# Attention times value on one core: output stores moved into the ring of the loads, and one more unit loaded in halves

## The chip, the cores and the metric

The kernel runs on one core of a Trainium2 chip. The metric is the device time of one execution in microseconds (us). The time of a run is some 2 us above the span of its profile (1064.05 against 1062.3 in the profiled run of the kernel before), which goes from the first to the last instruction.

## The reference

```python
# attn_weights: (8, 12, 1024, 1024) float32; v: (8, 12, 1024, 64) float32
return np.einsum('bhqs,bhsd->bhqd', attn_weights, v).astype(np.float32)
```

403 MB of attention weights and 25 MB of V are read, and 25 MB of output are written.

## The kernel before

Two heads make one unit ("pair"), so there are NP = 48 units. A unit's weights (8 MB of float32 in HBM) are loaded by a casting DMA that GpSimd issues, as 4 MB of bf16, into one of two buffers. PE transposes them, multiplies with V and transposes the result back; the unit's output (512 KB: 128 rows of 4 KB) is stored by a DMA that SP issues. In the profile the packets of the loads are on queue 0 (11520 packets; "the ring" in this document) and those of SP's DMAs on queue 1 (7520); the page counts 16 DMA engines.

```python
    HELD = 7
    MARK = 11
    chunks_of = {                          # how a unit's load is cut, in sixteenths
        NP - 3: [(0, GH), (GH, GH)],       # halves
        NP - 2: [(g, DG) for g in range(0, G, DG)],                       # quarters
        NP - 1: [(0, 4), (4, 4), (8, 4), (12, 2), (14, 1), (15, 1)],
    }
    o_pool = ctx.enter_context(tc.tile_pool(name="op", bufs=3 + HELD))
    # ... other pools cut

    def load_attn(ip):
        abf = abf_pool.tile([P, G, S], bf16)
        abf_of[ip] = abf
        for g0, gn in chunks_of.get(ip, [(0, G)]):
            nc.gpsimd.dma_start(
                out=abf[:, ds(g0, gn)].rearrange("p g s -> p (g s)"),
                in_=attn_p[ip][:, ds(g0 * S, gn * S)],
            )

    def store(ip, osb):
        nc.sync.dma_start(
            out=out_p[ip].rearrange("p g d -> p (g d)"),
            in_=osb.rearrange("p g d -> p (g d)"),
        )

    def store_held(abf, g):                # 7 stores wait for part of the last load
        mark = const_pool.tile([1, P], bf16)
        waits = nc.sync.dma_start(out=mark, in_=abf[0:1, g, 0:P])
        with tc.issue_after(waits.ins):
            for ip in sorted(held):
                store(ip, held.pop(ip))

    def pair(ip):                          # units 0 to 44
        # ... buffers cut
        for g in range(G):
            transpose_g(abf, at, g)
        load_ahead(ip)                     # the load of unit ip + 2 (and V every other time)
        # ... multiply, copies, transpose back cut
        if ip < NP - 1 - HELD:
            store(ip, osb)
        else:
            held[ip] = osb

    def direct_pair(ip, behind):           # units 45 to 47, a quarter at a time
        # ... cut
        if ip == NP - 1:
            store_held(abf, MARK)
        # ... per quarter: transposes, multiply, copies; unit 47 stores its pieces by SP
        load_ahead(ip)
        if ip < NP - 1:
            held[ip] = osb
```

Of the kernel before, what the change touches and what calls it, by code (L numbers as in the profile page):

```python
# [10 lines left out]
def kernel(  # L11
# [13 lines left out]
    nc = tc.nc  # L25
    fp32 = mybir.dt.float32
    bf16 = mybir.dt.bfloat16
# [4 lines left out]
    NP = NH // 2  # L32
    P = 128
    HP = P // 2
    G = Q // HP
    GH = G // 2
# [5 lines left out]
    NV = NH // VH  # L42


    HELD = 7
    MARK = 11
    DG = 4
    LAST = 3
    chunks_of = {
        NP - 3: [(0, GH), (GH, GH)],  # L50
        NP - 2: [(g, DG) for g in range(0, G, DG)],
        NP - 1: [(0, 4), (4, 4), (8, 4), (12, 2), (14, 1), (15, 1)],
# [8 lines left out]
    const_pool = ctx.enter_context(tc.tile_pool(name="const", bufs=1))  # L61
# [2 lines left out]
    vr_pool = ctx.enter_context(tc.tile_pool(name="vr", bufs=2))  # L64
    vbf_pool = ctx.enter_context(tc.tile_pool(name="vbf", bufs=4))
    ot_pool = ctx.enter_context(tc.tile_pool(name="ot", bufs=2))
    o_pool = ctx.enter_context(tc.tile_pool(name="op", bufs=3 + HELD))
    pt_pool = ctx.enter_context(tc.tile_pool(name="pt", bufs=4, space=bass.MemoryType.PSUM))
    po_pool = ctx.enter_context(tc.tile_pool(name="po", bufs=2, space=bass.MemoryType.PSUM))
    px_pool = ctx.enter_context(tc.tile_pool(name="px", bufs=2, space=bass.MemoryType.PSUM))  # L70
# [32 lines left out]
    def load_attn(ip):  # L103
        abf = abf_pool.tile([P, G, S], bf16)
        abf_of[ip] = abf
        for g0, gn in chunks_of.get(ip, [(0, G)]):
            nc.gpsimd.dma_start(  # L107
                out=abf[:, ds(g0, gn)].rearrange("p g s -> p (g s)"),
                in_=attn_p[ip][:, ds(g0 * S, gn * S)],
            )  # L110

    def load_first_v():
        v32 = const_pool.tile([P, VB, SB * D], fp32)
        nc.sync.dma_start(out=v32.rearrange("p b x -> p (b x)"), in_=v_g[0])
        vr = vr_pool.tile([P, VB, SB * D], bf16)
        vr_of[0] = vr
        nc.vector.tensor_copy(out=vr, in_=v32)  # L117

    def load_v(iv):
        vr = vr_pool.tile([P, VB, SB * D], bf16)  # L120
        vr_of[iv] = vr
        nc.gpsimd.dma_start(out=vr.rearrange("p b x -> p (b x)"), in_=v_g[iv])  # L122
# [21 lines left out]
    def transpose_g(abf, at, g):  # L144
        pt = pt_pool.tile([P, KW, P], fp32)
        words = abf[:, g].bitcast(fp32).rearrange("p (c k) -> p k c", k=KW)
        for k in range(KW):
            nc.tensor.matmul(  # L148
                out=pt[:, k],
                lhsT=words[:, k],  # L150
                rhs=ident,
                is_transpose=True,
                start=(k == 0),
                stop=(k == KW - 1),
            )
        copy = nc.vector.tensor_copy if g % 8 in (0, 2, 4, 5, 7) else nc.scalar.copy
        copy(  # L157
            out=at[:, g].rearrange("c k j two -> c (k j two)"),
            in_=pt.rearrange("c k j -> c (k j)").bitcast(bf16),
        )  # L160
# [20 lines left out]
    def transpose_back(ot, o_halves, j0, jn):  # L181
        px = px_pool.tile([P, jn, P], fp32)
        for j in range(jn):
            last = nc.tensor.matmul(  # L184
                out=px[:, j],
                lhsT=ot[:, j0 + j].rearrange("p h q -> p (h q)"),
                rhs=ident,
                is_transpose=True,
                start=(j == 0),
                stop=(j == jn - 1),  # L190
            )
        nc.scalar.copy(  # L192
            out=o_halves[:, :, ds(j0, jn)].rearrange("p half j d -> p j half d"),
            in_=px.rearrange("p j (half d) -> p j half d", half=2),
        )
        return last

    held = {}

    def store(ip, osb):  # L200
        nc.sync.dma_start(
            out=out_p[ip].rearrange("p g d -> p (g d)"),
            in_=osb.rearrange("p g d -> p (g d)"),
        )

    def store_held(abf, g):

        mark = const_pool.tile([1, P], bf16)
        waits = nc.sync.dma_start(out=mark, in_=abf[0:1, g, 0:P])
        with tc.issue_after(waits.ins):  # L210
            for ip in sorted(held):
                store(ip, held.pop(ip))

    def pair(ip):
        abf = abf_of.pop(ip)
        at = at_pool.tile([P, G, KW, P, 2], bf16)
        vbf = vbf_of.pop(ip)
        po = [po_pool.tile([P, GH * HP], fp32, name="po") for h in range(2)]
        ot = ot_pool.tile([P, GH, 2, HP], fp32)
        osb = o_pool.tile([P, G, D], fp32)  # L220
        o_halves = osb.rearrange("p (half j) d -> p half j d", half=2)
# [4 lines that stand above are left out]
        for h in range(2):  # L226
            for half in range(2):
                multiply(at, vbf, po, h, half)
        to_sbuf(po, ot)
        if ip % 2 == 0 and ip // 2 + 1 < NV:  # L230
            spread_v(ip // 2 + 1)
        for j0 in (0, 4):
            last = transpose_back(ot, o_halves, j0, 4)
# [4 lines that stand above are left out]
        return last  # L238

    def direct_pair(ip, behind):  # L240

        abf = abf_of.pop(ip)
        at = at_pool.tile([P, G, KW, P, 2], bf16)
        vbf = vbf_of.pop(ip)
        osb = o_pool.tile([P, G, D], fp32)
        if ip == NP - 1:
            store_held(abf, MARK)
        for c0, cn in chunks_of[ip]:
            for g0 in range(c0, c0 + cn, DG):
                gn = min(DG, c0 + cn - g0)  # L250
                with tc.issue_after(behind.ins):
                    for g in range(g0, g0 + gn):
                        transpose_g(abf, at, g)
                px = px_pool.tile([P, gn, 2, D], fp32)
                for g in range(g0, g0 + gn):
                    n = 0
                    for kw in range(KW):
                        for par in range(2):
                            behind = nc.tensor.matmul(  # L259
                                out=px[:, g - g0].rearrange("p h d -> p (h d)"),  # L260
                                lhsT=at[:, g, kw, :, par],
                                rhs=vbf[:, 2 * kw + par].rearrange("p h d -> p (h d)"),
                                start=(n == 0),
                                stop=(n == SB - 1),
                            )
                            n += 1
                for h in range(2):
                    copy = nc.vector.tensor_copy if h == 0 else nc.scalar.copy
                    rows = ds(h * HP, HP)
                    copy(out=osb[rows, ds(g0, gn)], in_=px[rows, :, h])  # L270
                if ip == NP - 1 and g0 in stores_of:
                    gs = ds(*stores_of[g0])
                    nc.sync.dma_start(out=out_p[ip][:, gs], in_=osb[:, gs])
        load_ahead(ip)
        if ip < NP - 1:
            held[ip] = osb
        return behind

    def load_ahead(ip):


        nxt = ip + 2
        if nxt < NP:
            if nxt % 2 == 1 and (nxt + 1) // 2 < NV:
                load_v((nxt + 1) // 2)
            load_attn(nxt)

    load_attn(0)
    load_first_v()
    constants()  # L290
    load_v(1)
    load_attn(1)
    spread_v(0)
    for ip in range(NP - LAST):
        last = pair(ip)
    for ip in range(NP - LAST, NP):
        last = direct_pair(ip, last)
# [30 lines left out]
```

## Time and profile before

| | before |
|---|---|
| time, median (lowest to highest), as known at the prediction | 1065.76 us (1063.76 to 1065.77) |
| span of the profiled run | 1062.3 us |
| PE busy | 76% |
| loads in the ring, share of 16 DMA engines | 93.9% |
| SP's queue (stores, first V) | 6.5% |

From the page of the kernel before: busy time of PE with its share of the span, the DMA engines' busy tenths in 40 equal slices, and the queues (packets, MB, share of 16 engines' time).

```profile
PE 806.8 (76%) x5640; PEld 648.9 (61%) x5640; DVE 390.1 (37%) x590; ACT 399.0 (38%) x486; POOL 46.3 (4%) x89
...
DMA  9999999999999999999999999999999999999998
...
q0 software_dynamic: 11520, 213.39, 93.9%
q1 hardware_dynamic: 7520, 26.22, 6.5%
q8 instruction: 44, 0.72, 0.2%
q14 instruction: 12, 0.10, 0.0%
```

The DMA engines are the limit.

The chain of waits of the kernel before, from 840 us on (start, length, what):

```profile
960.75 29.60 DMA abf<-in_attn_weights_dram
990.34 0.14 issue
990.48 1.53 PE pt L148 x6
992.01 1.71 PE px L184 x8
993.71 7.73 PE pt L148 x58
1001.44 4.74 PE po L167 x32
...
1052.28 0.55 PE pt L148 x4
```

The fourth unit from the end lands whole at 990.34; from there the chain is PE work, with short copies between, until the end. PE is late, and so is the last load, which must wait until the transposes of unit 45 have freed its buffer. The timeline of GpSimd in the kernel before (start, length; in brackets the idle time before it and what ended that):

```profile
1024.38 3.18 POOL L107 DMA_DIRECT2D abf<-in_attn_weights_dram  x6 [20.53 <-PE pt L148]
```

Stretches of the tail of the kernel before. The last two columns are the DMA engines' mean busy share and the GB/s they wrote:

```profile
core 0: us, PE busy (x) PEld busy (x) DVE busy (x) ACT busy (x) POOL busy (x), PEclk, DMA share, GB/s
1022.00:1026.00 4.00, 4.00 (x53) 3.99 (x52) 2.49 (x5) 1.38 (x2) 1.62 (x4) 1.00 0.84 160
...
1050.00:1054.00 4.00, 3.70 (x52) 3.50 (x51) 2.25 (x4) 1.91 (x3) 0.00 (x0) 1.00 1.03 411
1054.00:1058.00 4.00, 2.51 (x28) 1.98 (x25) 0.93 (x4) 1.48 (x3) 0.00 (x0) 1.00 1.00 393
1058.00:1060.00 2.00, 0.62 (x8) 0.45 (x8) 0.62 (x2) 0.21 (x1) 0.00 (x0) 1.00 0.29 100
```

The engines dip to 0.84 at 1022 to 1026, and they drain the held stores at full share until 1058.

### The profile page before, as it was taken

The numbers are of one execution on the slowest core, as the hardware profiler recorded it, in microseconds if no ns is written. First come the engines' busy times: TensorE is split into PE (matmuls) and PEld (weight loads), VectorE is DVE, ScalarE is ACT, GpSimd is POOL, SyncE is SP. The second block draws the span as 40 slices with busy tenths as digits, with TensorE's granted clock in tenths as the row PEclk, the third lists the DMA queues.
The fourth block names the chain that finished last, engine by engine and source line by source line (L and its number), as shares of the span: only waits on it lengthen the run. The fifth ranks groups of instructions, "written<-read, shape, count | busy, mean of one in ns | idle before, by whom it ended". The sixth has DMA issues, their size and how long they took to land.

```text
span 1062.3 us, 12938 instructions
## 1 busy us (share of the span) xinstructions
PE 806.8 (76%) x5640; PEld 648.9 (61%) x5640; DVE 390.1 (37%) x590; ACT 399.0 (38%) x486; POOL 46.3 (4%) x89
## 2 busy tenths in 40 slices
PE   0988758787688876777668787788777877688797
PEld 0676546665567655665556655666556655577597
DVE  0353323433234333343334433344333433334354
ACT  0353324433244332443324433344333433334353
POOL 2000000000000000000000000000000000000010
PEclk9988878888888887888878888778877888878899
DMA  9999999999999999999999999999999999999998
GB/s 215 220 221 239 225 220 236 228 223 232 225 229 229 225 225 239 221 221 238 227 225 229 230 224 229 227 228 230 222 230 236 221 222 233 233 217 217 208 202 253
DMA packets 19096, 240.43 MB, mean 226 GB/s; under 512 B 2144, under 2 KB 2528, under 8 KB 12000
## 3 DMA queue, kind: packets, MB, share of 16 engines
q0 software_dynamic: 11520, 213.39, 93.9%
q1 hardware_dynamic: 7520, 26.22, 6.5%
q8 instruction: 44, 0.72, 0.2%
q14 instruction: 12, 0.10, 0.0%
HBM read 427.82 MB, written 25.17 MB: 426 GB/s over the span
## 4 chain that ended last, share of the span: by engine, by line
DMA 69%; issue 20%; PE 10%; DVE 0%; ACT 0%; POOLq 0%
DMA abf<-in_attn_weights_dram 69%; PE pt L148 6%; PE px L259 2%; PE px L134 1%; PE px L184 1%; PE po L167 0%; DVE vbf L142 0%; DVE at L157 0%; ACT at L157 0%; DVE osb L270 0%; ACT osb L270 0%; POOLq L107 0%; POOLq L122 0%; POOLq L77 0%; POOLq L312 0%
## 5 line engine op out<-in xcount | busy, mean ns | idle before, releaser
L148 PE MATMUL pt<-ident,abf 128*128 128x128 f32 x3072 | 455.2, 314 | 214.2 <-DMA abf<-in_attn_weights_dram 214.2
L148 PEld LDWEIGHTS pt<-ident,abf 128*128 128x128 f32 x3072 | 436.7, 214 | 232.8 <-issue 157.9
L157 DVE COPY at<-pt 128x1024 bf16<-128x1024 bf16 x480 | 319.0, 688 | 448.9 <-PE pt L148 446.2
L157 ACT COPY at<-pt 128x1024 bf16<-128x1024 bf16 x288 | 288.3, 1013 | 107.4 <-PE pt L148 106.5
L167 PE MATMUL po<-at,vbf 128*64 128x512 bf16 x1440 | 216.5, 391 | 0.0
L167 PEld LDWEIGHTS <-vbf 128*64 128x64 bf16 x1440 | 106.5, 108 | 92.9
L192 ACT COPY osb<-px 128x512 f32<-128x512 f32 x90 | 52.6, 585 | 276.5 <-PE px L184 276.4
L179 ACT COPY ot<-po 128x512 f32<-128x512 f32 x45 | 26.3, 585 | 191.4 <-PE po L167 191.4
L184 PE MATMUL px<-ident,ot 128*128 128x128 f32 x360 | 84.5, 396 | 17.4 <-DVE vbf L142 17.4
L184 PEld LDWEIGHTS px<-ident,ot 128*128 128x128 f32 x360 | 69.3, 211 | 28.7 <-DVE vbf L142 28.7
L142 DVE CAST vbf<-px 128x512 bf16<-128x512 f32 x48 | 33.2, 691 | 96.0 <-PE px L134 96.0
L179 DVE COPY ot<-po 128x512 f32<-128x512 f32 x45 | 31.1, 691 | 100.7 <-PE po L167 100.7
L107 POOL DMA_DIRECT2D abf<-in_attn_weights_dram x57 | 31.2, 552 | 840.5 <-PE pt L148 839.7
L134 PE MATMUL px<-vr,spread 32*128 32x512 bf16 x384 | 53.8, 386 | 18.5 <-DVE vbf L142 18.5
L142 ACT CAST vbf<-px 128x512 bf16<-128x512 f32 x48 | 28.1, 585 | 63.9 <-PE px L134 63.9
L134 PEld LDWEIGHTS <-spread 32*128 32x128 bf16 x384 | 17.2, 93 | 52.5 <-issue 43.0
L259 PE MATMUL px<-vbf,at 128*128 128x128 bf16 x384 | 23.9, 219 | 2.3 <-ACT at L157 1.2
L259 PEld LDWEIGHTS <-at 128*128 128x128 bf16 x384 | 22.5, 98 | 3.1 <-DVE at L157 1.5
L122 POOL DMA_DIRECT2D vr<-in_v_dram x23 | 12.2, 530 | 140.2 <-PE px L134 140.2
L270 ACT COPY osb<-px 64x256 f32<-64x256 f32 (+2 forms) x14 | 4.7, 336 | 20.6 <-DVE osb L270 20.6
L270 DVE COPY osb<-px 64x256 f32<-64x256 f32 (+2 forms) x14 | 5.3, 378 | 18.4 <-PE px L259 18.4
L117 DVE CAST vr<-v 128x2048 bf16<-128x2048 f32 x1 | 1.2, 1226 | 4.4 <-DMA v<-in_v_dram 4.4
(9 smaller groups left out, 4.9 us busy)
## 6 DMA issues: line engine op xcount, KB each, us to landing
abf<-in_attn_weights_dram POOLq DMA_DIRECT2D x45, 4096.0 KB, 33.0
out_dram<-osb SPq DMA_DIRECT2D x47, 512.0 KB, 19.6
vr<-in_v_dram POOLq DMA_DIRECT2D x23, 512.0 KB, 27.9
abf<-in_attn_weights_dram POOLq DMA_DIRECT2D x7, 1024.0 KB, 17.4
abf<-in_attn_weights_dram POOLq DMA_DIRECT2D x2, 2048.0 KB, 23.3
v<-in_v_dram SPq DMA_DIRECT2D x1, 1024.0 KB, 4.9
abf<-in_attn_weights_dram POOLq DMA_DIRECT2D x1, 512.0 KB, 21.5
abf<-in_attn_weights_dram POOLq DMA_DIRECT2D x2, 256.0 KB, 22.6
```

What stands on the lines that cost most here:

```text
L107: nc.gpsimd.dma_start(out=abf[:, ds(g0, gn)].rearrange("p g s -> p (g s)"), in_=attn_p[ip][:, ds(g0 * S, gn * S)],)
L122: nc.gpsimd.dma_start(out=vr.rearrange("p b x -> p (b x)"), in_=v_g[iv])
L134: nc.tensor.matmul(out=px, lhsT=spread[rows, b], rhs=vr[rows, b], start=(b == 0), stop=(b == VB - 1),)
L142: copy(out=vbf[:, :, h % 2], in_=px.rearrange("p (k d) -> p k d", k=SB))
L148: nc.tensor.matmul(out=pt[:, k], lhsT=words[:, k], rhs=ident, is_transpose=True, start=(k == 0), stop=(k == KW - 1),)
L157: copy(out=at[:, g].rearrange("c k j two -> c (k j two)"), in_=pt.rearrange("c k j -> c (k j)").bitcast(bf16),)
L167: nc.tensor.matmul(out=po[h][ds(half * D, D)], lhsT=vbf[:, 2 * kw + par, h], rhs=at[:, ds(half * GH, GH), kw, ds(h * HP, HP), par], start= ...
L179: copy(out=ot[:, :, h], in_=po[h].rearrange("p (j q) -> p j q", j=GH))
L184: last = nc.tensor.matmul(out=px[:, j], lhsT=ot[:, j0 + j].rearrange("p h q -> p (h q)"), rhs=ident, is_transpose=True, start=(j == 0), st ...
L192: nc.scalar.copy(out=o_halves[:, :, ds(j0, jn)].rearrange("p half j d -> p j half d"), in_=px.rearrange("p j (half d) -> p j half d", half=2),
L259: behind = nc.tensor.matmul(out=px[:, g - g0].rearrange("p h d -> p (h d)"), lhsT=at[:, g, kw, :, par], rhs=vbf[:, 2 * kw + par].rearrange ...
L270: copy(out=osb[rows, ds(g0, gn)], in_=px[rows, :, h])
```

## The change

It wants three things: cheaper stores (issued by GpSimd into the ring of the loads, the 8 rows of each engine flagged as one packet), a tail in which six held stores stand strictly behind the last load, and an earlier start for PE in the tail (unit 44 loaded in halves). The core of the diff:

```diff
     HELD = 7
-    MARK = 11
     chunks_of = {
+        NP - 4: [(0, GH), (GH, GH)],
         NP - 3: [(0, GH), (GH, GH)],
@@
-    o_pool = ctx.enter_context(tc.tile_pool(name="op", bufs=3 + HELD))
+    o_pool = ctx.enter_context(tc.tile_pool(name="op", bufs=4 + HELD))
@@ def store(ip, osb):
-        nc.sync.dma_start(
+        nc.gpsimd.dma_start(
             out=out_p[ip].rearrange("p g d -> p (g d)"),
             in_=osb.rearrange("p g d -> p (g d)"),
+            single_packet=True,
         )
-    def store_held(abf, g):
-        ...
@@ def direct_pair
-        if ip == NP - 1:
-            store_held(abf, MARK)
@@
-        load_ahead(ip)
         if ip < NP - 1:
             held[ip] = osb
+        load_ahead(ip)
+        if ip == NP - 2:
+            store(ip, held.pop(ip))
@@ def load_ahead(ip):
-            load_attn(nxt)
+            last = load_attn(nxt)
+            if nxt == NP - 1:
+                with tc.issue_after(last.ins):
+                    for n in sorted(held):
+                        store(n, held.pop(n))
```

The last unit's four pieces stay with SP.

More of the change, by code (lines that the diff above doesn't have):

```diff
@@ L106, in load_attn @@
         for g0, gn in chunks_of.get(ip, [(0, G)]):
-            nc.gpsimd.dma_start(
+            last = nc.gpsimd.dma_start(
                 out=abf[:, ds(g0, gn)].rearrange("p g s -> p (g s)"),
@@ L110, in load_attn @@
             )
+        return last
     def load_first_v():
@@ L200, in store @@
     def store(ip, osb):
-        nc.sync.dma_start(
+        nc.gpsimd.dma_start(
             out=out_p[ip].rearrange("p g d -> p (g d)"),
             in_=osb.rearrange("p g d -> p (g d)"),
+            single_packet=True,
         )
-    def store_held(abf, g):
-        mark = const_pool.tile([1, P], bf16)
-        waits = nc.sync.dma_start(out=mark, in_=abf[0:1, g, 0:P])
-        with tc.issue_after(waits.ins):
-            for ip in sorted(held):
-                store(ip, held.pop(ip))
     def pair(ip):
```

## The prediction

> **What bounds it now.** The DMA engines. The DMA row of the 40-slice table is 9 in every slice but the last; the queue table gives the software ring (loads) 93.9% and the hardware queue (stores) 6.5% of 16 engines, while PE is busy 76%. In the chain of waits two units take 44.0 us (mean of 17 such periods). In the trace's packet records a packet of a whole load (64 KB read, 32 KB written) takes 2434 ns: 27 bytes read per ns, 431 GB/s for 16 engines.[...] Two loads cost 38.6 us of every 44.0, the V load 2.6, two stores the other 2.7: 1.36 us each.
>
> From 990 us the chain of waits is PE alone: the fourth unit from the end lands whole at 990.4, its 64 transposes run until 1001.4, and PE has no gap until 1052. So the last unit's loads are issued only at 1024.4, and the packet records show engines partly idle at 1022 to 1026.5, worth 1.1 us of all 16. The last loads end near 1048.5; seven held stores and the last pieces drain until about 1058; the last small store lands at 1062.
>
> **What the change does.**
> 1. 40 stores move from their own queue into the ring of the loads, 8 rows per engine in one packet; bytes are unchanged. A 4 KB store packet takes 172 ns among loads; at 27 bytes per ns it would be 151. Load packets of 4 to 64 KB read fit 20 ns plus bytes/27, so I take 20 ns as a packet's cost. [...] this trace has 12% on 4 KB. Estimate: 7 of 8 overheads saved, 0.14 us per store, 5 us in all. Against it: [...] each store puts a completion write among the loads. I count -4, between -6 and +4.
> 2. GpSimd waits for a store's result before the next load, but that result is ready some 8 us before that load may be issued: no loss. The added buffer covers the longer latency.
> 3. The halved load lets PE transpose the first half about 10 us earlier. PE's chain moves forward 5 to 6 us, the last unit's loads are issued near 1018, and the idle patch goes: -1.1 us. PE then waits for loads in the last units, so only part of its gain shows.
> 4. Six stores stand behind the last load instead of seven racing its last quarter; 0.4 us of idle near 1046 goes. Loads end near 1047; eight stores' data (1.25 us each) drain until 1057, end about 1058: -3.5 us for the tail in all. The drain, not PE, ends it.
>
> **Predicted time.** 1065 - 4 - 3.5, about 1057.5 us; range 1051 to 1066. Faster by over 2%: 0.02[...]; within 2%: 0.94; slower: 0.04.
>
> **What would show it.** Right: a period of 43.7 us; store packets of 152 to 158 ns in the software ring, hardware queue share near 0.5%; PE waiting for attention loads in the last two units; no DMA dip near 1022. Wrong: ring store packets of 172 ns or more, or a DMA dip at each store.
>
> **What would make it wrong.** [...] If the last small stores, on the other queue, must alternate with 32 KB packets of the ring, they land late and eat the tail's gain. If interleaving already hid the packet cost, only the tail's 3 us remains.

Passages that rest on figures or mechanisms which no trace of this case shows are cut; the cuts are marked. The sum came to 1065 - 4 - 3.5, about 1057.5 us. Its -4 was an estimate of 5 us from the trace's packet times, less an allowance. The 20 ns of step 1 come from the medians of the trace before: 173, 324, 625, 1227 and 2431 ns for load packets of 4, 8, 16, 32 and 64 KB read. The 12% are 20 of the 172 ns of a store packet.

## More of the kernel before

Most run times of the kernel before lie near 1063.7 or near 1065.8, with some between (1064.2 to 1064.6); nothing here explains this scatter. It is as large as several of the effects below, and it is why a gain by the medians and one by the ratio of means can differ by almost 1 us. The profiled run of the kernel before (1064.05) belongs to the lower group.

## The result, and the profile after

| | before | after |
|---|---|---|
| time, median (lowest to highest) of 4 runs each | 1064.76 us (1063.61 to 1065.77) | 1061.55 us (1061.27 to 1062.20) |
| ratio, 95% interval | | 0.9971 [0.9954, 0.9988] |
| span of the profiled run | 1062.3 us | 1059.6 us |

A ratio in this document is the mean time of one kernel's runs over that of the other's of the same rounds, so it is not quite the ratio of the medians. The gain is real and small: about 3 us, where 7.5 were predicted.

From the page after, the lines that answer to those of before:

```profile
PE 808.4 (76%) x5640; PEld 645.0 (61%) x5640; DVE 390.7 (37%) x590; ACT 399.6 (38%) x486; POOL 71.8 (7%) x137
...
DMA  9999999999999999999999999999999999999998
...
q0 software_dynamic: 18432, 238.03, 100.0%
q1 hardware_dynamic: 720, 1.57, 0.4%
q8 instruction: 44, 0.72, 0.2%
q14 instruction: 12, 0.10, 0.0%
```

The stores have moved to queue 0, and the DMA engines are as full as before. The chain of waits after, from 1000 us on:

```profile
977.51 30.19 DMA abf<-in_attn_weights_dram
1007.70 0.14 issue
1007.84 2.17 PE pt L150 x16
1010.01 1.79 PE px L252 x32
1011.80 2.00 PE pt L150 x16
1013.80 0.28 issue
1014.08 1.04 POOL abf L108 x2
1015.12 27.74 DMA abf<-in_attn_weights_dram
1042.86 0.14 issue
1042.99 2.17 PE pt L150 x16
```

PE is no longer late. The last load is issued at 1014.08, and the chain goes through DMAs again, as predicted. The stretches of the tail after:

```profile
1022.00:1026.00 4.00, 3.59 (x46) 3.44 (x43) 1.86 (x4) 1.61 (x3) 0.54 (x1) 1.00 1.05 219
...
1050.00:1054.00 4.00, 1.81 (x21) 1.42 (x20) 1.10 (x3) 1.33 (x3) 0.00 (x0) 1.00 0.64 253
1054.00:1058.00 4.00, 0.00 (x0) 0.00 (x0) 0.02 (x1) 0.21 (x1) 0.00 (x0) 0.74 0.38 148
1058.00:1060.00 2.00, 0.00 (x0) 0.00 (x0) 0.00 (x0) 0.00 (x0) 0.00 (x0) 0.50 0.00 0
```

The dip at 1022 is gone. But the drain, which ran at full share before, now runs at 0.64 and 0.38 for 8 us. From 1050 to 1058, half of the DMA engines' time is empty, PE has nothing left to do, and yet the program is not over. This is where the expected gain is missing.

The trace says more of the empty engines. It records the time of each update of a DMA's semaphore: in either kernel 2128 updates by 133 DMAs, 16 each, and as many packets of 4 bytes (the prediction's completion writes; 1280 of them on queue 0 before, 2048 after). That each of the 16 tells of the landing of one engine's share is my reading; in a_four below, a store of 4 rows has 4 such packets. So I take the 16 as a load's landing times. For two loads, in us (first, 8th, 9th and last of the 16):

```
                  42nd load                       last load (last sixteenth of unit 47)
          first   8th    9th    last              first    8th      9th      last
before    923.4   926.6  928.5  929.6             1046.66  1047.01  1048.75  1049.98
after     918.0   921.1  922.6  924.2             1040.49  1043.34  1046.26  1048.58
```

The sixteen engines do not march together. Some run 6 us behind others by the 42nd load, in both kernels (6.2 us from the first to the last landing, for 1.4 and 1.9 us at the 6th). (The landings are sorted; the trace does not number the engines.) In the kernel after, the first engine has the last load 6.2 us earlier than in the kernel before, and the last engine only 1.4 us earlier. The leading engines then finish their stores and stand empty, while the lagging ones set the end: the last engine's share of the last big store lands at 1057.84, that of the last small one at 1058.04.

### The profile page after: what moved, and what is told of

Read it like the earlier page. It is cut to its first block, busy times and chain, and to the rows that moved or that the text cites. A ratio compares the mean times of both kernels' runs of the same rounds, so it can differ in the third digit from the quotient of the medians.

```text
span 1059.6 us, 12899 instructions
## 1 busy us (share of the span) xinstructions
PE 808.4 (76%) x5640; PEld 645.0 (61%) x5640; DVE 390.7 (37%) x590; ACT 399.6 (38%) x486; POOL 71.8 (7%) x137
## 2 busy tenths in 40 slices
DMA packets 19208, 240.43 MB, mean 227 GB/s; under 512 B 2128, under 2 KB 2512, under 8 KB 11984
## 4 chain that ended last, share of the span: by engine, by line
DMA 73%; issue 14%; PE 9%; POOL 2%; ACT 1%; DVE 0%; POOLq 0%
DMA abf<-in_attn_weights_dram 73%; PE pt L150 5%; PE px L186 2%; ACT osb L194 1%; POOL vr L124 1%; POOL out_dram L203 1%; PE px L136 1%; PE px L252 1%; PE po L169 0%; DVE vbf L144 0%; POOL abf L108 0%; DVE at L159 0%; ACT at L159 0%; DVE osb L263 0%; ACT osb L263 0%
## 5 line engine op out<-in xcount | busy, mean ns | idle before, releaser
L150 PE MATMUL pt<-ident,abf 128*128 128x128 f32 x3072 | 463.2, 319 | 194.3 <-DMA abf<-in_attn_weights_dram 194.3
L150 PEld LDWEIGHTS pt<-ident,abf 128*128 128x128 f32 x3072 | 449.7, 214 | 209.4 <-issue 116.3
L186 PE MATMUL px<-ident,ot 128*128 128x128 f32 x360 | 69.8, 340 | 30.3 <-DVE vbf L144 17.4
L186 PEld LDWEIGHTS px<-ident,ot 128*128 128x128 f32 x360 | 52.8, 174 | 50.7 <-DVE vbf L144 28.7
L203 POOL DMA_DIRECT2D out_dram<-osb x47 | 25.2, 536 | 462.8 <-ACT osb L194 424.8
```

The source lines that it names most:

```text
L150: nc.tensor.matmul(out=pt[:, k], lhsT=words[:, k], rhs=ident, is_transpose=True, start=(k == 0), stop=(k == KW - 1),)
L186: last = nc.tensor.matmul(out=px[:, j], lhsT=ot[:, j0 + j].rearrange("p h q -> p (h q)"), rhs=ident, is_transpose=True, start=(j == 0), st ...
L203: nc.gpsimd.dma_start(out=out_p[ip].rearrange("p g d -> p (g d)"), in_=osb.rearrange("p g d -> p (g d)"), single_packet=True,)
```

## The experiments

Two theories went into the runs. **Theory A (lag):** one half of the DMA engines carries PE's instruction fetches besides the data (the 44 packets of queue 8, 16 KB and about 940 ns each) and falls behind; the slowest engine sets the end, and the dip at 1022 was in the leading engines alone. **Theory B:** the engines are alike, the prediction's sum holds, and something else in the new tail takes the gain back. Nine kernels ran, each on one chip; all gave correct results. "Slowest landing" is the last of the 16 landings of the last load. A pair of medians from different calls compares runs on different chips; the kernel before had medians of 1064.76, 1063.84, 1064.00 and 1064.24 there.

### One part alone: the halves (b_split)

```diff
 # on the kernel before
+        NP - 4: [(0, GH), (GH, GH)],
```

> The kernel before with the fourth unit from the end loaded in halves and nothing else. Theory A (lag): half of the DMA engines run some 6 us behind the others, they never idled in the kernel before, and the idle patch of 1.1 us was in the leading half alone. Then the patch goes, but the lagging engines end as before: what is won is only what PE's chain was later than the lagging engines' last stores, about 1 us (span 1061.3, between 1060.7 and 1062). Theory B (the prediction's sum: the patch is worth 1.1 us and PE's lateness the rest of the tail's 3.5): 2.5 to 3.5 us faster, span near 1059.3.

Measured: 1063.31 us against 1063.84, ratio 0.9987 [0.9975, 1.0]; span 1061.6. The stretch that had the dip:

```profile
1022.00:1026.00 4.00, 4.00 (x52) 3.99 (x52) 2.08 (x4) 2.49 (x4) 1.03 (x2) 1.00 1.04 217
```

The dip is filled (1.04 for 0.84), and the span is only 0.7 us shorter. The last load's landings say why: the first engine is at 1042.92 instead of 1046.66, and the slowest at 1050.37 instead of 1049.98. The filled dip helped engines that were not the limit. The span fits A (1060.7 to 1062) and not B (near 1059.3).

### One part alone: the 40 early stores in the ring (b_ring)

```diff
 # on the kernel before; the held stores and the mark stay with SP
+    bufs=4 + HELD
         if ip < NP - 1 - HELD:
-            store(ip, osb)
+            nc.gpsimd.dma_start(out=..., in_=..., single_packet=True)
```

> The kernel before with the 40 early stores alone moved to GpSimd, one packet per engine, in the ring of the loads; the tail stays on the other queue behind the mark, the fourth unit from the end stays whole. The landings of after against before drift apart by 0.058 us per store between the 6th and the 42nd load, which would make 2.3 us for 40. Theory A: 2 to 2.5 us faster (span near 1060), nearly all of the whole change. Theory B (0.1 to 0.14 us per store, taken back by the tail): 4 to 5.5 us faster (span near 1057.5).

Measured: 1061.91 us against 1063.84, ratio 0.9975 [0.9961, 0.9988]; span 1060.1. About 2 to 2.7 us, most of the whole change, and half of what the optimistic reading asked for.

### The one-packet flag taken away (a_nopacket)

```diff
 # on the kernel after
-            single_packet=True,
```

> The changed kernel without the one-packet flag; stores stay in the ring. If the 0.058 us per store come from the packet (overhead saved 7 times of 8 per engine), the store records go from 159 back to about 172 ns and 2 to 3 us are lost again (span 1061.5 to 1062.5). If they come from the single ring[...], nothing changes (span 1059.6 within 0.5).

Measured: 1061.66 us (1061.35 to 1062.67), ratio to before 0.9974; span 1059.9. In the trace's packet records, 4 KB store packets in the ring take 159 ns with the flag and 159 ns without it; on SP's queue among loads they took 172 ns. These are medians: in the ring, with or without the flag, the first of the eight packets that an engine gets of a store takes 172 ns and the other seven 159; on SP's queue seven of eight take 172, mostly behind a load packet, and from 1049 us on, when hardly a load is left, most take 159 there too. So the flag does nothing that these runs can see, and what gain there is comes from the ring. My reading of 20 ns per packet as something that the flag removes fell here.

### All of the change without "six behind the last load" (b_ring_split)

```diff
 # b_ring, plus
+        NP - 4: [(0, GH), (GH, GH)],
```

> The kernel before with the 40 early stores in the ring of the loads and the fourth unit from the end in halves; the last stores stay on the SP queue behind the mark. It is the change without its 'six behind the last load'. If that part is worth nothing, this equals the changed kernel within 0.6 us (span 1059.3 to 1060.3); if it gives the 1 to 1.5 us that the prediction counted for it, this is slower than the changed kernel by that much (span 1060.6 to 1061.1). Last load's landing: first engine near 1040, last near 1048.6, as in the changed kernel.

Measured: 1061.49 us (1060.64 to 1061.64), ratio 0.9966 [0.9954, 0.9979]; span 1059.7; landings of the last load 1040.69 first and 1048.66 last. It equals the changed kernel (1061.55, span 1059.6). Putting the held stores behind the last load in the ring gave nothing.

### The halves undone (a_whole)

```diff
 # on the kernel after
-        NP - 4: [(0, GH), (GH, GH)],
```

> The changed kernel with the fourth unit from the end loaded whole again. Theory A (lag): the lagging engines' loads are not held up by PE, so the drain stays as it is; PE's chain moves back by 5 to 6 us, its last small store then lands about 1 us after the lagging engines' last store. 0.3 to 1.2 us slower (span 1060 to 1061). Theory B (the halves bring the tail's gain by closing the idle patch): 2 us slower or more (span 1061.6 and up).

Measured: 1062.75 us (1062.35 to 1063.64), ratio 0.9988 [0.9976, 1.0001]. By the medians this is 1.2 us above the changed kernel, the upper edge of what A expected and short of B's 2 us; by the ratios to the kernel before (0.9988 against 0.9971) it is 1.8 us, so this run alone does not part the theories. b_ring against b_ring_split, the same edit with the other tail and on other chips, gives 0.4 us by the medians and 0.9 by the ratios. The profiled run is the slowest of the five (span 1061.9), and its slowest engine was already 1.2 us later at the 42nd load (925.4 against 924.2), before the edited unit. So the profile alone would overstate the halves. Such a start differs by about 1 us from run to run; that the fetches fall differently on the engines is my guess at why, and not tested. The last small store landed 0.2 us after the last big one, where A had expected about 1 us.

### The same bytes, uneven over the engines (a_uneven)

Pieces of 8 rows were expected to load 8 engines, always the same ones.

```diff
 # on the kernel after, store(ip) for ip = 0, 4, ... 36
+   rows 0..95   : nc.gpsimd.dma_start(..., single_packet=True)    # meant: 6 rows on each of 16 engines
+   rows 96..127 : 4 x nc.sync.dma_start(8 rows)                   # meant: one row on each of 8 engines
```

> The changed kernel, but 10 of the 40 early stores move only rows 0 to 95 by GpSimd over all 16 engines, and rows 96 to 127 by SP in pieces of 8 rows, which should run on 8 engines only; same bytes in all. One half of the engines gets about 0.31 us more per such store, the other 0.31 us less, 3.1 us in sum. Theory A (lagging half sets the end): 1.5 to 3 us faster if the eight are the leading half, about 3 us slower if they are the lagging half; the spread of the landings of the last load goes from 8 us to about 2, or to about 14. Theory B (engines are alike, the tail waits for something else): within 0.7 us, and no such change of the spread.

What the traces show of it: the semaphore of an 8-row piece has 9 updates here and that of a 4-row piece 5 in a_four, one more than the 8 and 4 engines expected, where that of each DMA of the changed kernel has 16; and the 32 pieces of a_four bring 128 more packets of 4 bytes, four a piece. That the pieces always reach the same engines is assumption, and the trace can't show it.

Measured: 1064.77 us (1063.94 to 1067.10), ratio 1.0004; span 1061.7. Same bytes, and 3.1 us slower than the flagless kernel. The slowest landing of the last load went from 1048.58 to 1050.80, while the mean landing of the 42nd load moved by only 0.3 us. The expectation of "all leading or all lagging" missed: the eight are, by the reading below, a mixture. The landings of the 42nd load, as differences from their mean, in order:

```
after      -3.0 -3.0 -3.0 -2.8 -2.7 -2.6 -1.7  0.2 | 1.6  1.6  1.8  1.8  2.8  2.8  3.0  3.2
a_uneven   -5.3 -5.3 -2.1 -1.7 -0.7 -0.6 -0.4  0.3   0.4  0.5  0.6  0.6  1.5  2.9  4.6  4.8
a_pad      -4.3 -4.2 -4.1 -4.0 -3.8 -3.6 -2.9 -2.0 | 2.3  2.7  2.9  2.9  4.3  4.3  4.5  5.2
a_four     -4.3 -4.2 -4.1 -4.1  0.2  0.3  0.4  0.4   1.2  1.3  1.4  1.5  1.6  2.0  2.5  3.9
```

In the first line there are two groups of eight. By estimate, with ten uneven stores the eight engines that take pieces should move by about +3.2 (20 rows of 4 KB, 159 ns each) and the other eight by -3.2. I read the table so: two engines at -5.3 were leading and got less, two at +4.7 were lagging and got more, and the rest met in the middle; of the eight engines six were leading and two lagging. By this arithmetic the two that were lagging and got more ended the program. That many small stores by SP are not what costs the time follows from a_four below, which has 32 of them to the 40 here and loses nothing.

### The suspected cost added: more instruction fetches (a_pad)

```diff
 # on the kernel after, in front of each back-transpose of units 0 to 39
+        for _ in range(26):                       # twice a unit; overwritten at once
+            nc.tensor.matmul(out=px[0:32, 0, 0:32], lhsT=spread[:, 0, 0:32],
+                             rhs=spread[:, 0, 0:32], start=True, stop=True)
```

> The changed kernel with 4160 further PE instructions in the first 40 units (52 tiny bf16 matmuls a unit, overwritten at once; PE has some 6 us of idle time in each), so the same data and about 16 more instruction fetches of 16 KB. Theory A (each fetch is one packet of about 0.95 us on one of eight engines): two more per lagging engine, 1.6 to 2.2 us slower (span near 1061.5), while the first engine's landings of the last load stay where they were (1040.5) and the spread of the last load grows from 8 to about 10 us. Theory B (the fetches spread over all 16 engines, or cost only their bytes): 0.27 MB more of 454 MB, 0.6 us, spread unchanged.

Measured: 1064.79 us (1064.22 to 1064.99), ratio 1.0005; span 1063.2. That is 3.2 us slower than the changed kernel. The queue table of this run:

```profile
q0 software_dynamic: 18432, 238.03, 99.7%
q1 hardware_dynamic: 720, 1.57, 0.4%
q8 instruction: 60, 0.98, 0.3%
q14 instruction: 12, 0.10, 0.0%
```

4160 more PE instructions made 16 more packets on queue 8 (60 for 44), that is 260 instructions a packet. The data is the same to the packet. In the table above the two groups of eight went further apart: their medians differed by 5.0 us, and now by 7.5, so two more fetches per lagging engine, by estimate (16 packets over eight engines), cost about 1.2 us each, somewhat more than the packet's own 940 ns. The spread of the 42nd load grew from 6.2 to 9.5 us.

The mechanism is A's, but my size was too small (1.6 to 2.2 us). The slowest landing of the last load is 3.6 us later (1052.16 for 1048.58). I did not expect the leading engine to move too: its landing of the last load went from 1040.49 to 1044.89. In the tail the leading engines ran out of work: the first half of unit 45 was issued at 983.37 (977.00 in the changed kernel), when the first engine had landed all before it (982.81), and it landed there 13.3 us after that, where a half takes 9.7. The fetches' bytes alone, 0.26 MB, would by estimate take 0.6 us of all 16 engines at the 431 GB/s of the trace before.

A rival is that the extra instructions made PE late. The trace speaks against it: from unit 2 to unit 43 PE starts the transposes of a unit 0.04 to 0.14 us after the unit has landed, as in the changed kernel, and from the fifth load to the last each load is issued more than 8 us before the slowest engine has landed the one before it.

The kept traces also show which engines the fetches fall on. In the changed kernel, from the 6th load to the 42nd, 32 packets of queue 8 run. From one load to the next, the landings of the lagging eight, counted from the first landing, slip by about 1.1 us for each of these packets (34.9 us in sum), one engine at a time. Six of the leading eight keep within 0.5 us of each other all the while. The other two slip too, in steps of 0.3 to 1.0 us, together 4.1 us; each of these seven steps falls in a load with an 8 KB packet of queue 14, which was not followed up.

### The lag taken away, two tries (a_six, a_four)

```diff
 # a_six: 16 of the 40 early stores; rows 0..111 by GpSimd, rows 112..127 by SP in pieces of 6, 6, 4
 # a_four: 8 of the 40 early stores; rows 0..111 by GpSimd, rows 112..127 by SP in 4 pieces of 4
```

> The changed kernel, but 16 of the 40 early stores move only rows 0 to 111 by GpSimd over all 16 engines, and rows 112 to 127 by SP in pieces of 6, 6 and 4 rows. From the uneven run I read that 6 of the 8 engines that took its pieces were leading and 2 lagging[...]. Theory A: lagging engines get 16 rows less of 4 KB, 2.5 us in sum, so the spread of the last load falls from 8 to about 5 to 6 us and the program is 1.8 to 2.6 us faster (span near 1057.3). If the six are not all leading, it is slower by about 1 to 2 us, as the uneven run was. Theory B: unchanged within 0.5.

Measured: 1062.82 us (1062.74 to 1064.08), ratio 0.9990: 1.3 us slower than the changed kernel. The slowest landing of the last load rose to 1050.78, from 1048.58. By my reading the engines that took the pieces were not all leading; which engines a piece reaches was an assumption. This is the branch of the expectation that named 1 to 2 us.

> The changed kernel, but 8 of the 40 early stores move rows 112 to 127 by SP in four pieces of 4 rows each, the rest by GpSimd as before. From the landings of the two uneven runs, the four engines that take such pieces are all leading ones; they get 24 rows more of 4 KB in all (about 3.8 us), the other twelve 8 rows less (1.25 us). Theory A (the lagging engines set the end): the last engine's landing of the last load is 1.0 to 1.4 us earlier and the program 0.8 to 1.4 us faster than the changed kernel (span 1058.2 to 1058.8). If nothing but the total of bytes counts: unchanged within 0.4.

Measured: 1060.80 us (1060.75 to 1061.12), ratio 0.9962 [0.9948, 0.9976]; span 1058.9. By the median it is the fastest kernel here: 0.7 us below b_ring_split on the same chip, and below every run of the changed kernel (lowest 1061.27), though that was another chip. The gain is not clear of noise: one of the five runs of b_ring_split, 1060.64, is below all of a_four's, and the intervals of the two ratios overlap. The table shows what happened: the four leading engines that took no pieces went from about -3.0 to -4.2, the lagging ones from 1.6..3.2 to about 1.2..2.5. The slowest landing of the last load is 1047.91, 0.67 us earlier for 1.0 to 1.4 expected. One engine stands alone at 3.9. By the arithmetic it is the one at 0.2 in the changed kernel, which was among the four and got 24 rows more (3.8 us); that is an inference, as the trace does not number the engines. The stretches of the tail of this kernel:

```profile
1050.00:1054.00 4.00, 1.78 (x20) 1.42 (x20) 1.13 (x3) 0.98 (x3) 0.00 (x0) 1.00 0.80 317
1054.00:1058.00 4.00, 0.00 (x0) 0.00 (x0) 0.00 (x0) 0.00 (x0) 0.00 (x0) 0.52 0.27 103
```

The same work is packed closer: 0.80 for 0.64, and then 0.27 for 0.38. A finer balance would have some more of this to gain; it was not tried.

## Why the prediction was right or wrong

**Right.** The kernel is bound by DMA (the 431 GB/s of the prediction are bytes read, of which half as many are written into SBUF; the page has 426 GB/s over the whole span, and what sets the figure is not shown here), its time stays within 2%, and 1061.55 us lies in the range given, which was 15 us wide. PE's lateness goes, the dip at 1022 goes, PE waits for loads in the last units again, and the share of SP's queue falls to 0.4%. The drain, not PE, ends the program. GpSimd's waits for store results (446.7 us in 43 waits) cost nothing that the trace shows: the ring's share is 100.0%. A big store takes 20.0 us to land at the median and 28.8 at most, for 19.6 and 24.9 before. The DMA dip at each store that was named as a sign against it did not come, nor did the last small store end the program by alternating with ring packets: it landed 0.2 us after the last big one, though the four small ones took 7.3, 6.1, 5.5 and 3.8 us to land, for 5.7, 4.5, 3.6 and 1.6 before. Of the other signs named, the period is 43.84 us by the slowest landings (43.7 named) and a store packet in the ring takes 159 ns (152 to 158 named).

**Wrong: the gain.** It was to be 7.5 us and is 3.1. Two terms of the sum failed.

*Step 1, "two stores the other 2.7: 1.36 us each ... I count -4".* Measured, the early stores in the ring alone are worth 2 to 2.7 us (b_ring), and the flag nothing (a_nopacket). The sum took 20 ns off seven of eight packets, 0.14 us per store; the record shows 13 ns (172 to 159) on six of eight, flag or no flag. The 1.36 us, from which the sum seemed to have room for this, was mis-sized as well, as I took the period of two units, 44.0 us, from the landing of the whole load, which is that of the slowest engine. Between the 6th and the 42nd load the slowest landings advance by 43.97 us per period and the first landings by 43.70 us; the difference is the growing lag, not the stores. With two loads at 38.6 and V at 2.6 us, the first engine leaves about 1.25 us per store, and its period after the change is 43.60 (43.84 by the slowest landings). So 0.05 to 0.06 us per store, 2.1 to 2.6 us for 40, is what the ring won; at the 27 bytes per ns of the load packets a store's 32 KB per engine need, by estimate, 1.21 us anyway. Why a store packet behind a load packet takes 172 ns and one behind another store packet 159 ns stays open.

*Steps 3 and 4, "the idle patch goes: -1.1 us" and "-3.5 us for the tail in all".* These took the 16 engines for one. The patch was a mean over 16 engines, but it lay in the leading ones: the first of them had landed unit 46 at 1023.4 and had no work until the last load was issued at 1024.4, while the slowest still landed unit 46 at 1030.1. The slowest engine did not wait there: in the kernel before its landings of the quarters around the dip are 1024.5, 1030.1, 1034.9 and 1039.8, at most one fetch above the 4.9 us of a quarter. Filling the dip moved the first landing of the last load by 3.7 us and the slowest by -0.4 us, i.e. later (b_split). What the halves could win was PE's own lateness at the very end: in the kernel before, the last small store, which waits for PE, landed at 1061.19, 1.1 us after all the others (1060.05). The halves alone gave 0.5 us by the medians and 1.4 by the ratio, and the order of the last stores gave nothing (b_ring_split against after). What was expected of the tail went into idle time of the leading engines: shares of 0.64 and 0.38 in the last 8 us.

**What is shown and what is not.** That the slowest engine sets the end is shown in one direction: the same bytes spread worse cost 3.1 us (a_uneven). The other direction, the same bytes spread better (a_four), agrees by its landings and its median, 0.7 us, but is not clear of noise. That instruction fetches make the lag is shown by a_pad, and by the landings that slip with each packet of queue 8. Why a fetch costs about 1.1 us where its packet takes 0.94 is open. Which engines lag was only narrowed down: eight of the sixteen by the landings, and by my reading of a_uneven two of them among the eight that its pieces reach. The scattered run times of the kernel before, and the last 1.5 us between the last landing and the end of the span (1.1 before), were not examined.

## What to carry to other kernels

In a kernel bound by DMA, do not treat 16 DMA engines as one: look at the first and the last of a load's landings, for the period and above all for the tail. An idle patch in the mean share of the engines is worth little if the engines that set the end were not in it, and a period taken from whole landings holds the growing lag as well as the work. Instructions are DMA traffic too: 4160 more of them on PE made 16 more packets of 16 KB and cost 3.2 us here, as much as the whole change won. Whether trimming a long PE program wins as much was not tried, and giving lagging engines less to store won 0.7 us, within the noise.
